# A one-core decoder block: reads of accumulators reordered, feature-major matmuls grouped by width, one gate block moved

## The chip, the cores and the metric

One core of a Trainium2 chip. The time is the device time of one execution in microseconds; lower is better. The kernel before took 669.32 us in the median of three runs (668.25 to 670.68).

## The reference

A decoder block over 256 tokens of width 2,048, float32 throughout. The input is RMS-normalised and goes through one wide projection, whose columns feed two mixers. One is an mLSTM with 4 heads of 256 (q and k pass a causal convolution of four taps and a SiLU, then chunks with gates); the other is sparse attention with 16 heads of 64 over 4 key groups (a compressed branch, a selected branch and a window branch). Each result is gated, both are joined, projected, and added to x.

```python
h = rmsnorm(x, norm_g[l])
(mq, mk, mv, mo, mz, mi, mf, nq, kc, vc, ks, vs, kw, vw, ng, nz) = split_cols(h @ w_in[l], IN_SPLITS)
...
hm = head_layernorm(hm, m_norm_g[l]).astype(x.dtype)
m_out = hm * jax.nn.sigmoid(mo) * jax.nn.silu(mz)
...
n_out = n_att * jax.nn.silu(nz)
x = x + jnp.concatenate([m_out, n_out], axis=-1) @ w_out[l]
ple = rmsnorm(p[l] @ ple_proj_w[l], ple_norm_g[l])
x = x + jax.nn.sigmoid(x @ ple_gate_w[l]) * ple
return rmsnorm(x, final_norm_g)
```

## The kernel before

**Blocks and units.** All weights are streamed once from DRAM in an order laid out by hand (`STREAM`, lines 54 to 65): cs, q0 to q2, kw, vw, mo, mv, qk0 to qk7, mz0 and mz1, then ple and nz in turn, out, gate. A block is a set of columns over the whole contraction; it is cut into units of one, two or four 128-row slices (`ku`). A unit is loaded on SP's queue (`load`, L155), split into a high part by ScalarE (L164) and a low part, the rest, by VectorE (L165), and multiplied by TensorE (`mm`). Each float32 product is made of three matmuls: high by high, high by low, low by high.

**Two forms.** A token-major block has the activations as the stationary operand and the weights as the moving one, up to 512 columns wide (L190). A feature-major block (qk0 to qk7, nz0 to nz3) has the weights stationary: per slice one matmul of 512 columns (high weights, both halves of the activations, L178) and one of 256 (low weights, high half, L179), in turn:

```python
for j in range(b.ku):
    ...
    PE.matmul(o, wh, b.xT(kt, True), start=kt == 0, stop=False, skip_group_check=True)
    PE.matmul(o[:, 0], wl, b.xT(kt)[0], start=False, stop=kt == b.nk - 1, skip_group_check=True)
```

**The order of the work.** The main loop (L1291) is one step per unit. A step evacuates the block that ended, loads the unit four ahead, splits the unit three ahead, multiplies its own unit, and calls `advance`, which gives every open track one turn, up to its next `yield`. Every engine runs its instructions in the order in which the steps issue them. Weights have four buffers, accumulators of the main kind three banks, of the aux kind two, of the wide kind one; two engines that read one accumulator tile are ordered one after the other as the program names them.

**The steps that matter here.**
- x_squares (L260) loads x in eight pieces on SP and squares them on ScalarE; norm_scale (L272) makes of the sums the scale rr (a power on GpSimd, L275) and its copies rh, rq and rb. The track starts in step 1, rope_tables (L326, a sine on ScalarE at L347) in step 11, split_w1 (L481, eight slices of the compression weights, L485 and L486) in step 15.
- After block cs, in step 16, split_v (L514) evacuates two accumulators: ScalarE reads the value half (L518), VectorE reads it (L519), then ScalarE reads the key half (`also`, L527). k_stack (L366) rotates the keys, splits them one step later into kst (L371, L372), and transposes them two steps after that (L383).
- nsa (L590) runs the attention in twelve rounds of five steps: scores, masked maximum (L695), exponentials (L706), a scaling on GpSimd (L717) that VectorE's L714 and L715 prepare, transposes (L729), the product with v.
- ev_qk and conv (L865, L882) evacuate a qk block and apply the convolution, mostly on VectorE (L893).
- mlstm (L918) starts after the last convolution. Per head there are three steps: e1 the exponentials, p1 the product into the wide bank (with p0, the scores of the next head), e2 the copy to hm (L963) and the statistics read from PSUM (L966, L967). Then all heads are normalised.
- ev_mz (L1014) evacuates an mz block and gate_m (L1029) multiplies the gates; when the heads are done it multiplies hm, transposes it in two groups (L1048) and evacuates each into mixm with ScalarE (L1053) and VectorE (L1054) in turn, each of the two groups of mz0 and mz1 through one aux bank.

## Time and profile before

| what | us |
|---|---|
| median of three runs | 669.32 |
| the profiled execution's own time | 668.31 |
| its span, first to last instruction | 666.6 |
| TensorE matmul busy (PE) | 645.2 |
| VectorE (DVE) / ScalarE (ACT) / GpSimd (POOL) busy | 456.0 / 378.6 / 62.6 |
| VectorE low parts of the weights, L165 | 258.6 |
| ScalarE high parts of the weights, L164 | 216.7 |

Matmuls are pipelined and their ends are modelled, so the busy time of TensorE overstates how long one takes; the distance between starts says more. PEld is the weight load, which overlaps. A number in brackets behind a timeline row is the idle time of the engine before it and what ended it. PEclk is the granted TensorE clock as a share of full speed.

### The profile page before, as it was taken

What the parts mean: (1) busy time and instruction counts of PE and PEld (TensorE: products, weight loads), DVE (VectorE), ACT (ScalarE), POOL (GpSimd) and SP (SyncE); (2) the same over time, 40 slices, a digit from 0 to 9 for tenths busy, and PEclk for the clock granted to TensorE, in tenths of its full rate; (3) what the DMA queues carried; (4) which work ended last, traced back from release to release, by engine and by line L of the source; (5) the groups of instructions that cost most, each with busy time, mean ns of one, the idle gap of its engine ahead of it and who ended that gap; (6) DMA issues with size and microseconds to landing.
All of it is one profiled execution on the core that took longest, in us unless ns stands there. A gap on an engine that the chain in (4) does not pass through costs nothing.

```text
span 666.6 us, 9325 instructions
## 1 busy us (share of the span) xinstructions
PE 645.2 (97%) x3423; PEld 555.6 (83%) x3423; DVE 456.0 (68%) x690; ACT 378.6 (57%) x647; POOL 62.6 (9%) x70
## 2 busy tenths in 40 slices
PE   7998999999999999999999999989999999999994
PEld 5887999998888888888878888868888888888884
DVE  4657788648666667999998565866655764545564
ACT  5757854665655547776666455667644434344442
POOL 0010230000111211111100000100000000022430
PEclk9999999999999999999999999989999999999998
DMA  8974555564555544444456535436588675566623
GB/s 286 387 284 140 165 174 168 150 213 147 169 154 160 160 139 147 137 149 134 150 176 192 186 126 156 154 115 207 179 273 297 197 235 180 186 188 191 188 96 127
DMA packets 36478, 121.05 MB, mean 182 GB/s; under 512 B 4304, under 2 KB 5072, under 8 KB 35920
## 3 DMA queue, kind: packets, MB, share of 16 engines
q1 hardware_dynamic: 35280, 115.98, 54.7%
q10 hardware_dynamic: 1152, 4.47, 1.9%
q8 instruction: 27, 0.44, 0.3%
q14 instruction: 19, 0.16, 0.1%
HBM read 118.33 MB, written 2.10 MB: 181 GB/s over the span
## 4 chain that ended last, share of the span: by engine, by line
PE 84%; DVE 8%; ACT 3%; issue 2%; DMA 1%; POOL 1%; SPq 0%; ACTq 0%; POOLq 0%
PE mainps L190 56%; PE mainps L178 10%; PE mainps L179 5%; DVE wlo L165 3%; PE wideps L190 3%; PE wideps L683 2%; PE auxps L729 1%; ACT whi L164 1%; DMA wraw<-in_wst_dram 1%; PE wideps L958 1%; PE po L762 1%; PE po L760 1%; PE auxps L1185 1%; PE auxps L933 1%; PE wideps L622 1%
## 5 line engine op out<-in xcount | busy, mean ns | idle before, releaser
L165 DVE TENSOR_TENSOR wlo<-wraw,whi 128x1024 fp32r<-128x1024 f32 (+3 forms) x218 | 258.6, 1187 | 175.5 <-ACT whi L164 171.7
L164 ACT CAST whi<-wraw 128x1024 fp32r<-128x1024 f32 (+3 forms) x218 | 216.7, 998 | 173.0 <-PE mainps L190 118.2
L190 PE MATMUL mainps<-whi,hT 128*128 128x512 f32 (+3 forms) x768 | 185.0, 361 | 2.9 <-ACT whi L164 1.4
L190 PEld LDWEIGHTS mainps<-whi,hT 128*128 128x128 f32 x768 | 131.1, 188 | 20.9 <-ACT whi L164 2.3
L178 PE MATMUL mainps<-hT,whi 128*128 128x512 f32 x384 | 137.6, 400 | 0.3 <-ACT ple L1109 0.3
L179 PE MATMUL mainps<-hT,wlo 128*128 128x256 f32 x384 | 107.9, 281 | 0.0
L190 PE MATMUL mainps<-wlo,hT 128*128 128x512 f32 (+3 forms) x384 | 106.6, 356 | 0.5 <-DVE wlo L165 0.5
L178 PEld LDWEIGHTS mainps<-hT,whi 128*128 128x128 f32 x384 | 72.5, 189 | 17.5 <-ACT ple L1109 0.6
L190 PEld LDWEIGHTS mainps<-wlo,hT 128*128 128x128 f32 x384 | 68.3, 188 | 9.9 <-DVE wlo L165 1.0
L179 PEld LDWEIGHTS mainps<-hT,wlo 128*128 128x128 f32 x384 | 72.8, 190 | 0.4
L190 PE MATMUL mainps<-whi,x2T 128*128 128x512 f32 (+1 forms) x288 | 70.4, 366 | 0.0
L190 PEld LDWEIGHTS mainps<-whi,x2T 128*128 128x128 f32 x288 | 50.8, 189 | 8.7
L717 POOL TENSOR_TENSOR pr<-pr,st 128x1024 f32<-128x1024 f32 x12 | 23.3, 1944 | 219.1 <-DVE st L715 219.1
L190 PE MATMUL mainps<-wlo,x2T 128*128 128x512 f32 (+1 forms) x144 | 41.0, 366 | 0.0
L190 PE MATMUL mainps<-whi,mixm 128*128 128x512 f32 x128 | 35.5, 399 | 0.0
L190 PE MATMUL mainps<-whi,mixn 128*128 128x512 f32 x128 | 34.2, 389 | 0.0
L190 PEld LDWEIGHTS mainps<-wlo,x2T 128*128 128x128 f32 x144 | 26.0, 189 | 4.5
L190 PEld LDWEIGHTS mainps<-whi,mixn 128*128 128x128 f32 x128 | 24.0, 188 | 5.1
L190 PEld LDWEIGHTS mainps<-whi,mixm 128*128 128x128 f32 x128 | 23.5, 188 | 5.1
L706 ACT ACTIVATE pr<-wideps,st 128x128 f32<-128x128 f32 (+1 forms) x64 | 26.5, 435 | 0.6 <-DVE st L695 0.6
L878 ACT COPY sc<-mainps 128x512 f32<-128x512 f32 x24 | 14.1, 586 | 17.5 <-PE mainps L179 17.4
L893 DVE SCALAR_TENSOR_TENSOR qk<-cv,csb,qk 128x253 f32<-128x253 f32 (+2 forms) x48 | 23.1, 481 | 1.1
(277 smaller groups left out, 707.5 us busy)
## 6 DMA issues: line engine op xcount, KB each, us to landing
wraw<-in_wst_dram SPq DMA_DIRECT2D x183, 512.0 KB, 3.7
wraw<-in_wst_dram SPq DMA_DIRECT2D x24, 344.0 KB, 3.2
wraw<-in_wst_dram SPq DMA_DIRECT2D x8, 304.0 KB, 2.9
xq<-in_x_dram SPq DMA_DIRECT2D x8, 256.0 KB, 8.5
w1raw<-in_w_dram SPq DMA_DIRECT2D x2, 1024.0 KB, 10.2
x<-in_x_dram ACTq DMA_DIRECT2D x4, 512.0 KB, 6.2
out_dram<-x SPq DMA_DIRECT2D x8, 256.0 KB, 2.7
xf<-in_xT_dram SPq DMA_DIRECT2D x3, 512.0 KB, 8.0
```

The costliest lines, as they stand in the source:

```text
L164: A.copy(hi[:, a:z], raw[:, a:z])
L165: V.tensor_tensor(lo[:, a:z], raw[:, a:z], hi[:, a:z].bitcast(F32), OP.subtract)
L178: PE.matmul(o, wh, b.xT(kt, True), start=kt == 0, stop=False, skip_group_check=True)
L179: PE.matmul(o[:, 0], wl, b.xT(kt)[0], start=False, stop=kt == b.nk - 1, skip_group_check=True)
L190: PE.matmul(b.ps[n], xx, (self.hi, self.lo)[part == 2][:, j, a:z], start=kt + part == 0, stop=part == 2 and kt == b.nk - 1)
L622: PE.matmul(psc[:, t, h].rearrange("p a c -> p (a c)"), qT[:, h, t * 128:(t + 1) * 128], kcmpT[:, h // NJ].rearrange("p a c -> p (a c)"), ...
L683: PE.matmul(ps[:, j], qT[:, g * NJ + j0 + j, t * 128:nk], kT[:, g, hl, :, 0:nk], start=hl == 0, stop=hl == 1)
L706: A.activation(d["pr"][:, j, b], d["ps"][:, j, b], AF.Exp, bias=st[:, 0, j, b:b + 1], accum_out=st[:, 1, j, b:b + 1])
L717: G.tensor_tensor(pf, pf, d["st"][:, 2].rearrange("p j b -> p (j b)")[:, :, None].to_broadcast([128, 2 * jn, nk]), OP.mult)
L729: PE.transpose(pt[:, s, j], d["pr"][:, j, b, s * 128:(s + 1) * 128], ident)
L878: A.copy(sc, ps[m])
L893: V.scalar_tensor_tensor(y[:, d:S], a[:, 0:S - d], w(j), y[:, d:S], op0=OP.mult, op1=OP.add)
```

## The change

Nine edits. In `mm`, the four slices' wide matmuls of a feature-major unit come first, then the four narrow ones. In split_v the call `also` stands before VectorE's read, and in gate_m both ScalarE reads stand before both VectorE reads. k_stack has one more yield before kst. The block mz0 moves ahead of the qk blocks, and the track ple_in opens with mz1. In mlstm the copy of a head is issued together with the exponentials of the next, its statistics are read from the SBUF copy hm one step later, and a head takes two steps. x_squares starts in step 3, rope_tables in step 10, split_w1 in step 13. The mv tile is 2,112 words instead of 2,056, and lg moves from the constants into the slot of bst.

```diff
@@ -56,8 +56,9 @@
 STREAM += [("kw", "w_in", span(C_KW, 256), KT, 4), ("vw", "w_in", span(C_VW, 304), KT, 2)]
 STREAM += [(f"mo{i}", "w_in", span(C_MO + i * 512, 512), KT, 2) for i in range(2)]
 STREAM += [(f"mv{i}", "w_in", span(C_MV + i * 512, 512), KT, 2) for i in range(2)]
+STREAM += [("mz0", "w_in", span(C_MZ, 512), KT, 2)]
 STREAM += [(f"qk{i}", "w_in", span(C_MQ + i * 256, 256), KT, 4) for i in range(8)]
-STREAM += [(f"mz{i}", "w_in", span(C_MZ + i * 512, 512), KT, 2) for i in range(2)]
+STREAM += [("mz1", "w_in", span(C_MZ + 512, 512), KT, 2)]
 for i in range(4):
     STREAM += [(f"ple{i}", "ple_proj_w", span(i * 512, 512), 2, 2)]
     STREAM += [(f"nz{i}", "w_in", span(C_NZ + i * 256, 256), KT, 4)]
@@ -171,12 +172,13 @@
             if b.feat:
                 for m in range(b.W // 128):
                     o = b.ps[m]
-                    for j in range(b.ku):
-                        kt = self.ka + j
-                        wh = self.hi[:, j, m * 128:(m + 1) * 128]
-                        wl = self.lo[:, j, m * 128:(m + 1) * 128]
-                        PE.matmul(o, wh, b.xT(kt, True), start=kt == 0, stop=False, skip_group_check=True)
-                        PE.matmul(o[:, 0], wl, b.xT(kt)[0], start=False, stop=kt == b.nk - 1, skip_group_check=True)
+                    ks = range(self.ka, self.ka + b.ku)
+                    for j, kt in enumerate(ks):
+                        PE.matmul(o, self.hi[:, j, m * 128:(m + 1) * 128], b.xT(kt, True), start=kt == 0, stop=False,
+                                  skip_group_check=True)
+                    for j, kt in enumerate(ks):
+                        PE.matmul(o[:, 0], self.lo[:, j, m * 128:(m + 1) * 128], b.xT(kt)[0], start=False,
+                                  stop=kt == b.nk - 1, skip_group_check=True)
                 return
             ns = range(len(b.cuts)) if ns is None else ns
             order = [(n, part) for n in ns for part in range(3)]
@@ -366,6 +368,7 @@
     def k_stack(kx, b):
         rope(kx.rearrange("p t (g d) -> p t g d", d=ND), NG)
         yield
+        yield
         kst = tmp.tile([128, T * NG, 2, 2, ND], F32R, name="kst", tag="hm")
         kb = kx.rearrange("p t (g d) -> p (t g) d", d=ND)[:, :, None, :].to_broadcast([128, T * NG, 2, ND])
         A.copy(kst[:, :, 0], kb)
@@ -516,9 +519,9 @@
         for t in range(T):
             v = ps_v[t].rearrange("p (g d) -> p g d", d=ND)
             A.activation(vs[:, t, :, 0], v, AF.Copy, scale=rr[:, t:t + 1])
+            also(t)
             V.scalar_tensor_tensor(vs[:, t, :, 1], v, rr[:, t:t + 1], vs[:, t, :, 0].bitcast(F32),
                                    op0=OP.mult, op1=OP.subtract)
-            also(t)
         vst[b] = vs
 
     def ev_s(ps):
@@ -807,7 +810,7 @@
         zz = zif.rearrange("p t (a h) -> p t a h", a=2)
         V.tensor_tensor(zz, zz, b_if[:, None].to_broadcast([128, T, 2, MH]), OP.add)
         zf = zz[:, :, 1]
-        lg = const.tile([128, 4, T, MH], F32, name="lg")
+        lg = tmp.tile([128, 4, T, MH], F32, name="lg", tag="bst")
         e, u, u2, ac = (lg[:, i] for i in range(4))
         V.scalar_tensor_tensor(e, zf, -1.0, zf, op0=OP.mult, op1=OP.max)
         A.activation(e, e, AF.Exp, scale=-1.0)
@@ -899,13 +902,16 @@
         if i == 7:
             tracks.append(mlstm())
 
+
+    MV_WORDS = 2112
     mv = None
 
     def ev_mv(i):
         def f(ps):
             nonlocal mv
             if i == 0:
-                mv = tmp.tile([128, T, MH, MD + 1], F32, name="mv", tag="mv")
+                mv = tmp.tile([128, MV_WORDS], F32, name="mv", tag="mv")[:, 0:T * MH * (MD + 1)]
+                mv = mv.rearrange("p (t h d) -> p t h d", t=T, h=MH)
                 G.memset(mv[:, :, :, MD:MD + 1], 1.0)
             for t in range(T):
                 A.activation(mv[:, t, 2 * i:2 * i + 2, 0:MD], ps[t].rearrange("p (h d) -> p h d", d=MD), AF.Copy,
@@ -962,21 +968,28 @@
             pn = sv[h]
             A.copy(hm[:, :, h], pn[:, :, 0:MD])
             V.tensor_copy(den[:, 0, :, h:h + 1], pn[:, :, MD:MD + 1])
+
+        def e3(h):
             for t in range(T):
-                V.bn_stats(bst[:, t, h], pn[:, t, 0:MD])
+                V.bn_stats(bst[:, t, h], hm[:, t, h])
                 V.bn_aggr(mva[:, t, h], bst[:, t, h])
 
         p0(0)
         yield
         for h in range(MH):
+            if h:
+                e2(h - 1)
             e1(h)
             yield
             p1(h)
             if h + 1 < MH:
                 p0(h + 1)
-            yield
-            e2(h)
-            yield
+            if h:
+                e3(h - 1)
+            yield
+        e2(MH - 1)
+        e3(MH - 1)
+        yield
         dd, rv, sh = den[:, 0], den[:, 1], den[:, 2]
         V.scalar_tensor_tensor(dd, dd, -1.0, dd, op0=OP.mult, op1=OP.max)
         V.tensor_scalar(dd, dd, 1.0, None, op0=OP.max)
@@ -1048,10 +1061,10 @@
                     PE.transpose(ps[:, j, t * 128:(t + 1) * 128], hf[:, t, (k0 + j) * 128:(k0 + j + 1) * 128], ident)
             yield
             for j in range(2):
-                hi, lo = mixm[:, 0, k0 + j], mixm[:, 1, k0 + j]
-                g = mgcol[:, k0 + j:k0 + j + 1]
-                A.activation(hi, ps[:, j], AF.Copy, scale=g)
-                V.scalar_tensor_tensor(lo, ps[:, j], g, hi.bitcast(F32), op0=OP.mult, op1=OP.subtract)
+                A.activation(mixm[:, 0, k0 + j], ps[:, j], AF.Copy, scale=mgcol[:, k0 + j:k0 + j + 1])
+            for j in range(2):
+                V.scalar_tensor_tensor(mixm[:, 1, k0 + j], ps[:, j], mgcol[:, k0 + j:k0 + j + 1],
+                                       mixm[:, 0, k0 + j].bitcast(F32), op0=OP.mult, op1=OP.subtract)
         done.add(f"mix{i}")
 
     def ev_nz(i):
@@ -1258,14 +1271,14 @@
     pb = [Block(f"ple{i}", ev_ple(i), p_of) for i in range(4)]
     mo, mz, nz = ([Block(f"{c}{i}", f(i), h_of, feat=c == "nz") for i in range(n)]
                   for c, f, n in (("mo", ev_mo, 2), ("mz", ev_mz, 2), ("nz", ev_nz, 4)))
-    blocks += mo + mv_b + qk_b + mz
+    blocks += mo + mv_b + mz[0:1] + qk_b + mz[1:2]
     for i in range(4):
         blocks += [pb[i], nz[i]]
     blocks += [Block(f"out{i}", ev_out(i), mix_of) for i in range(4)]
     blocks += [Block(f"gate{i}", ev_gate(i), x2_of, cuts=EDGES if i == 3 else None) for i in range(4)]
     assert [woff[n] for n, *_ in STREAM] == [b.off for b in blocks]
     units = [Unit(b, ka) for b in blocks for ka in range(0, b.nk, b.ku)]
-    ple_first = next(i for i, u in enumerate(units) if u.b is mz[0])
+    ple_first = next(i for i, u in enumerate(units) if u.b is mz[1])
     NU = len(units)
 
     first = ((512, 768), (768, 1024), (0, 512))
@@ -1304,15 +1317,16 @@
             load_x(8 + 4 * (i // 4), 12 + 4 * (i // 4))
             if i == 1:
                 nc.sync.dma_start(pos_i, positions)
-                tracks.append(x_squares())
+        elif i == 3:
+            tracks.append(x_squares())
         elif i in (6, 9):
             load_w1(i // 3 - 2)
-        elif i == 11:
+        elif i == 10:
             tracks.append(rope_tables())
         elif i == 12:
             nc.sync.dma_start(csb[:, 16:], cols[:, 16:N_COLS - 3 * ND])
             nc.sync.dma_start(boot, cols[:, N_COLS - 3 * ND:])
-        elif i == KT - 1:
+        elif i == 13:
             tracks.append(split_w1(w1r))
         elif i == KT + 2:
             tracks.append(masks())
```

## Rows read from the trace of the kernel before

**Rows 1.** The page, part 1: busy us (share of the span) xinstructions.

```profile
PE 645.2 (97%) x3423; PEld 555.6 (83%) x3423; DVE 456.0 (68%) x690; ACT 378.6 (57%) x647; POOL 62.6 (9%) x70
```

**Rows 2.** Windows: length, busy us (x) of each engine, PEclk, DMA share, GB/s.

```profile
52.00:56.00 4.00, 2.87 (x17) 2.46 (x16) 2.85 (x6) 1.95 (x6) 0.00 (x0) 1.00 0.83 240
140.00:332.00 192.00, 192.00 (x1043) 164.90 (x1042) 146.70 (x206) 119.55 (x254) 21.20 (x12) 1.00 0.49 152
332.00:336.00 4.00, 2.67 (x19) 2.21 (x18) 3.97 (x6) 3.10 (x5) 2.18 (x1) 1.00 0.57 182
436.00:440.00 4.00, 1.04 (x6) 0.68 (x6) 2.92 (x6) 2.11 (x5) 0.00 (x0) 0.83 0.68 227
440.00:444.00 4.00, 4.00 (x19) 3.59 (x20) 3.42 (x6) 1.45 (x4) 0.00 (x0) 0.74 0.22 45
```

**Rows 3.** Chain of waits: start us, us, what; 256-column kw, then 512-column blocks.

```profile
111.99 11.57 PE mainps L190 x96
...
145.78 2.84 PE mainps L190 x12
...
359.68 10.90 PE mainps L190 x48
```

**Rows 4.** Waits: engine line waited for: us in total, times, longest us.

```profile
ACT trig L347 <- DVE akk L345: 3.7, 1, 3.7
...
ACT kx L527 <- DVE vst L519: 2.0, 2, 1.5
```

**Rows 5.** Timeline of TensorE, block nz0: start us, us, engine line op [idle before].

```profile
417.52 0.39 PE L178 MATMUL mainps<-hT,whi 128*128 128x512 f32 x1
...
428.81 1.11 PE L190 MATMUL mainps<-whi,pTt 128*128 128x512 f32 x4
```

**Rows 6.** Timeline 44 to 65 us, GpSimd, ScalarE, VectorE, TensorE.

```profile
46.34 0.71 POOL L275 TENSOR_TENSOR rr<-rr,mh 128x2 f32<-128x2 f32 x1 [44.97 <-DVE posf L328]
...
52.44 0.47 ACT L518 ACTIVATE vst<-mainps,rr 128x256 fp32r<-128x256 f32 x1
...
53.90 0.47 DVE L519 SCALAR_TENSOR_TENSOR vst<-mainps,rr,vst 128x256 fp32r<-128x256 f32 x1
...
54.40 0.47 ACT L527 ACTIVATE kx<-mainps,rr 128x256 f32<-128x256 f32 x1 [1.50 <-DVE vst L519]
...
57.59 0.79 ACT L164 CAST whi<-wraw 128x688 fp32r<-128x688 f32 x1
...
62.79 1.22 DVE L372 TENSOR_TENSOR kst<-kx,kst 128x1024 fp32r<-128x1024 f32 x1
...
64.07 0.37 PE L383 MATMUL auxps<-identr,kst 128*128 128x128 f32 x2 [1.83 <-DVE kst L372]
```

**Rows 7.** Timeline 332 to 336 us, VectorE and TensorE.

```profile
333.12 2.92 DVE L165 TENSOR_TENSOR wlo<-wraw,whi 128x1024 fp32r<-128x1024 f32 x1
...
335.01 1.09 PE L729 MATMUL auxps<-ident,pr 128*128 128x128 f32 x8 [1.33 <-POOL pr L717]
```

**Rows 8.** Timeline at the joint of mz0 and mz1, VectorE and TensorE.

```profile
387.40 0.69 DVE L1022 SCALAR_TENSOR_TENSOR tz<-tz,zc 128x512 f32<-128x512 f32 x1 [0.49 <-ACT zc L1021]
...
387.42 1.20 PE L190 MATMUL mainps<-whi,hT 128*128 128x512 f32 x4 [0.34 <-ACT zc L1021]
```

**Rows 9.** Timeline of VectorE, statistics of the last head.

```profile
412.97 0.42 DVE L966 BATCH_NORM_STATS2 bst<-wideps 128x6 f32<-128x256 f32 x1
```

**Rows 10.** Timeline 436 to 440 us, VectorE, ScalarE, TensorE.

```profile
436.90 0.48 DVE L1054 SCALAR_TENSOR_TENSOR mixm<-auxps,csb,mixm 128x256 fp32r<-128x256 f32 x1
437.41 0.84 ACT L1053 ACTIVATE mixm<-auxps,csb 128x256 fp32r<-128x256 f32 x2 [1.31 <-DVE mixm L1054]
437.92 0.88 DVE L1054 SCALAR_TENSOR_TENSOR mixm<-auxps,csb,mixm 128x256 fp32r<-128x256 f32 x2 [0.54 <-ACT mixm L1053]
...
438.55 0.99 PE L1048 MATMUL auxps<-ident,hm 128*128 128x128 f32 x4 [2.53 <-DVE mixm L1054]
...
439.96 1.08 PE L1048 MATMUL auxps<-ident,hm 128*128 128x128 f32 x4 [0.43 <-DVE mixm L1054]
```

## The prediction

> **What bounds the kernel now.** I read the page first: the matmul stream is busy for 645.2 of 666.6 us [rows 1]. The four-microsecond windows come second, because a share over the whole span hides the places where TensorE stands still. From 140 to 332 us TensorE has no idle time at all; the windows that matter are those that fall short [rows 2]. In 52-56 us 1.13 us are missing, in 332-336 us 1.33, in 436-440 us 2.96, and the window after that is full but was granted a clock of 0.74 in the mean, so part of it ran on the lower level of 1.2 GHz. With the wait of 1.83 us at 64 us [rows 6] those holes, some 7.3 us and a slow stretch behind the last, are what a reordering can win in the middle of the run. Elsewhere only fewer matmul nanoseconds would help, and those are read from the chain of waits: 48 matmuls of 512 columns in 10.90 us, 227 ns each, and 96 of 256 columns in 11.57 us, 120.5 ns each [rows 3].
>
> The waits [rows 4] name what ended an engine's idle time, and the timelines further down show in which order it came about.
>
> **The matmuls sorted by width.** Alternating, the 32 pairs of block nz0 start at 417.52 us and are followed at 428.81 us: 11.29 / 32 = 352.8 ns a pair [rows 5]. Runs of one width would cost 227 + 120.5 = 347.5 ns [rows 3]. There are 12 feature-major blocks of 32 pairs, so 384 x 5.3 ns = 2.0 us, if every neighbour had its own width. In a group of four and four two of eight joints still change width, so I take less than three quarters: **-1.4 us**, between -2.0 and +1.7 (if the wide ones then run as in the slower dozen of rows 3, 2.84 / 12 = 237 ns: 384 x 4.4 ns more than now). A second effect costs no matmul time: the first narrow matmul, which needs the low half from VectorE, moves back by three wide ones, 3 x 227 = 0.68 us of slack for a late VectorE.
>
> The Trainium skill, page "TensorE: Matmul & The Clock Gate", section "Back-to-back issue gap", gives N / 2.4 + 2.5 ns for a matmul on the full clock, 215.7 + 109.2 = 325 ns a pair in either order. By it this term would be zero and the sum 1.4 us higher; both rows lie above it, and the measured 352.8 against 347.5 decides.
>
> **The front, 52 to 64 us.** Today ScalarE reads the value half of an accumulator, VectorE reads it, and only then may ScalarE read the key half: kx waits 1.50 us for vst, the second time 0.5 more, 2.0 us in two waits [rows 4, 6]. TensorE's second q0 matmul group waits for the bank that this read frees. With both ScalarE reads first, the bank is free when the vst subtraction ends, 53.90 + 0.47 = 54.37 instead of 54.40 + 0.47 = 54.87, and ScalarE reaches the cast that stands at 57.59 us [rows 6] 2.0 us sooner. That cast is what VectorE idles for, and the key split kst (62.79 to 64.01) follows it without a gap. TensorE has waited 1.83 us for it when its transposes go on at 64.07 us [rows 6]. The added yield of k_stack makes the split come one unit later on ScalarE and VectorE (one weight split and one w1 slice, about 1.4 us of VectorE, go ahead of it) and the transposes one unit later on TensorE (12 matmuls of 344 columns, about 1.9 us); alone it gains some 0.5 us, with the 2.0 us of ScalarE it leaves nothing to wait for.
> The moved tracks point the same way. The rope tables' sine, for which ScalarE stands 3.7 us [rows 4], comes one step earlier, into time in which VectorE idles; the w1 slices start two steps earlier; the rb copy goes from ahead of the vst subtraction to behind it. The price is that the squares of x, their eight 256 KB loads on SP's queue and with them the scale rr come two steps later. The loads fall behind two weight loads that are needed sooner, so SP's queue loses nothing. GpSimd makes rr at 46.34 + 0.71 = 47.05 us; two steps of 12 wide matmuls (2.72 us each) later is 52.5, and the evacuation that reads it starts at 52.44 [rows 6]. That is no cover at today's pace; but VectorE's step 13, where rr is then made, runs late today behind ScalarE's 3.7 us stand, which goes, so I expect some 2 us of cover. Beyond it each microsecond would stand on TensorE. I take **-2.7 us** of the 1.13 + 1.83; bounds -3.0 and +0.5 (rr a microsecond late, and only the bank's earlier release won).
>
> **mz0 ahead of qk.** Eight units of 2.72 us go ahead, with their eight loads (1,024 elements a partition each, as qk's) in the same order on SP; no matmul is added. The attention steps, one step later through k_stack, then overlap some seven steps less with the convolution. In that overlap VectorE is full (3.97 of 4) and falls behind until TensorE waits 1.33 us for a GpSimd product whose scalars came late [rows 2, 7]; there too a split took 2.92 us beside GpSimd's. With the overlap 7 x 2.7 us shorter the lag should not get there: **-1.3 us**, bounds -1.4 and +1.3 (it happens once more, since mz0's own work now lies in the attention: four ScalarE reads and four VectorE products of 0.69 us [rows 8], in the first two steps of qk, where VectorE is not yet full and the units of 2.8 us cover them). At the joint of mz0 and mz1 TensorE waits 0.34 us for a copy that stood behind the exponentials of a mixed head [rows 8]; that joint is gone and the new ones have one more bank's time: **-0.3 us**.
>
> **The heads and the mix.** A head now takes two steps instead of three, and its statistics read the SBUF copy. One from PSUM takes 0.42 us [rows 9]; no row shows one from SBUF. All eight lie beside matmuls, so up to twice that or half of it costs nothing; were they uncovered, they would cost up to 3.4 us. The end of the heads comes three steps earlier, but the transposes of the mix meet the next ple block instead of this one, in the same place of the same five-step pattern. So I expect the hole again, shorter. Now its four evacuations alternate, ScalarE, VectorE, ScalarE, VectorE, each waiting for the other: TensorE, done with its matmuls at 436.0, goes on at 438.55 and again at 439.96 [rows 10]. With both ScalarE reads first, VectorE can run its four subtractions of 0.4 us (two take 0.88) from 436.90 on without a wait, done near 438.7: **-1.2 us**. Bounds 0 and -4.5 (the hole of 2.96 gone, and with it the slow clock behind it, 0.74 of full speed over 4 us [rows 2], worth about a microsecond of matmuls).
>
> The padded mv tile, the lg tile in a pool slot, and the gates read ahead of the split in vw change no queue that anything waits on: zero, covered by full TensorE windows.
>
> **Sum.** -1.4 - 2.7 - 1.3 - 0.3 - 1.2 = -6.9 us against the profiled execution's own 668.3 us: 661.4. That execution lies 1.0 us below the median of the runs shown (669.32), so on the median's side I predict **662.4 us**.
>
> **Rivals.**
> 1. The waits are not from the order of readers but from VectorE's load, so the order of reads alone wins nothing: kx then still waits, kst too. Against it stands that VectorE is named as the releaser of a ScalarE read of other columns [rows 4]. The front keeps -0.5, the mix 0: 662.4 + 2.2 + 1.2 = 665.8 us. Chance 0.15.
> 2. Holes move. VectorE's lag in the overlap of convolution and attention recurs at each of the roughly five remaining attention rounds, 1.3 us each, in place of the one: 662.4 + 1.3 + 5 x 1.3 = 670.2, about no change. For it: VectorE is full there [rows 2]. Against: with as much overlap the rounds before the last one passed without a hole, 140 to 332 us. Chance 0.10, counting smaller forms of it.
> 3. Slower: the padded tile moves every later buffer, and the wide matmuls read their operands more slowly. Place: all 1,536 token-major matmuls of 512 columns. Price: the same twelve take 2.84 us in one stretch and 12 x 227 = 2.72 in another [rows 3], 0.12 x 128 twelves = 15.4 us: 677.8. It decides from 0.055 us a twelve on, where it eats the whole gain. Against it: both values stand in one trace, in which no buffer moves. Chance 0.05.
> 4. The hole at the mix vanishes and the clock stays full: 662.4 - 3.3 = 659.1. Chance 0.15.
>
> **How the numbers follow.** The forecast itself has 0.55. The range reaches from rival 4 with the better end of the sorting, 658, to rival 1 and part of rival 2, 667; about 0.15 lies above it, 0.04 below. A measurement of this kernel can tell about 0.3% (2.0 us) from no change. Faster by more than that: forecast, rivals 1 and 4, a little of rival 2, 0.86; within it 0.08; slower 0.06.
>
> **What would show it.** In the profile after: kx no longer waits for vst; the windows from 52 to 64 us read nearly 4.00; no wait of the probability transposes for the GpSimd product; eight matmuls of a feature-major group in about 1.39 us instead of 1.41; the second transposes of the mix come about 1.2 us after the first's request, not 4. I am wrong if a window that is full now shows a hole, above all where rr is first read and in the heads under nz0, or if twelve wide matmuls take over 2.75 us throughout.

## The result, and the profile after

The changed kernel takes **657.62 us** in the median of four runs (657.20 to 658.03), beside 669.81 (668.25 to 670.68) for the kernel before on the same chip: a ratio of 0.9821, with an interval of 0.9800 to 0.9841. That is 12.2 us less; 6.9 were forecast, and the time lies 0.4 us under the low end of the range. The profiled execution took 657.20 us, span 655.2.

Page, part 1, of the changed kernel (answers to [rows 1]):

```profile
PE 641.0 (98%) x3423; PEld 554.7 (85%) x3423; DVE 456.1 (70%) x690; ACT 379.0 (58%) x647; POOL 62.5 (10%) x70
```

The same instructions on every engine, and 4.2 us less matmul busy time, so 7.2 of the 11.4 us of span are idle time that went. Windows (answer to [rows 2]):

```profile
50.00:54.00 4.00, 4.00 (x25) 3.65 (x24) 2.83 (x6) 3.85 (x11) 2.59 (x11) 1.00 0.67 208
58.00:62.00 4.00, 4.00 (x29) 3.98 (x29) 4.00 (x6) 3.08 (x6) 0.00 (x0) 1.00 0.61 176
140.00:330.00 190.00, 190.00 (x1006) 162.39 (x1005) 139.58 (x190) 116.49 (x246) 22.06 (x13) 1.00 0.49 152
330.00:334.00 4.00, 3.44 (x24) 2.98 (x23) 3.93 (x5) 1.65 (x3) 1.31 (x1) 1.00 0.45 141
440.00:444.00 4.00, 2.67 (x18) 2.15 (x16) 3.13 (x6) 4.00 (x9) 0.00 (x0) 1.00 0.46 150
444.00:448.00 4.00, 3.86 (x25) 3.54 (x26) 3.96 (x8) 3.23 (x7) 0.00 (x0) 1.00 0.60 156
```

Both holes of the front are gone, the one near 330 us is smaller (0.56 for 1.33), and the mix misses 1.47 us where it missed 2.96, with the full clock behind it. Timelines of the front, ScalarE, GpSimd, VectorE and TensorE (answer to [rows 6]):

```profile
45.43 0.22 ACT L349 ACTIVATE trig<-akk 128x32 f32<-128x32 f32 x1
...
49.65 0.47 ACT L521 ACTIVATE vst<-mainps,rr 128x256 fp32r<-128x256 f32 x1
50.02 0.46 ACT L530 ACTIVATE kx<-mainps,rr 128x256 f32<-128x256 f32 x1
...
48.00 1.09 POOL L277 TENSOR_TENSOR rr<-rr,mh 128x2 f32<-128x2 f32 x1 [46.63 <-DVE rr L276]
...
59.72 1.22 DVE L375 TENSOR_TENSOR kst<-kx,kst 128x1024 fp32r<-128x1024 f32 x1
...
61.13 0.45 PE L386 MATMUL auxps<-identr,kst 128*128 128x128 f32 x4
```

The sine and kx carry no bracket: nobody waits any more ([rows 4] had 3.7 and 2.0 us there). The scale rr is ready at 49.09, 0.56 us ahead of the first evacuation that reads it. TensorE asks for kst after it is done, 60.94. Then the wait near 330 us and the mix, TensorE, ScalarE and VectorE (answer to [rows 7, 10]):

```profile
331.36 1.09 PE L732 MATMUL auxps<-ident,pr 128*128 128x128 f32 x8 [0.56 <-POOL pr L720]
...
438.72 0.60 PE L1061 MATMUL auxps<-ident,hm 128*128 128x128 f32 x4
442.08 0.60 PE L1061 MATMUL auxps<-ident,hm 128*128 128x128 f32 x4
444.14 0.63 PE L1061 MATMUL auxps<-ident,hm 128*128 128x128 f32 x4 [1.47 <-DVE mixm L1066]
...
441.83 0.85 ACT L1064 ACTIVATE mixm<-auxps,csb 128x256 fp32r<-128x256 f32 x2
442.56 1.06 ACT L165 CAST whi<-wraw 128x1024 fp32r<-128x1024 f32 x1
443.49 0.87 ACT L1064 ACTIVATE mixm<-auxps,csb 128x256 fp32r<-128x256 f32 x2
...
441.98 1.22 DVE L166 TENSOR_TENSOR wlo<-wraw,whi 128x1024 fp32r<-128x1024 f32 x1 [0.87 <-ACT whi L165]
443.12 0.87 DVE L1066 SCALAR_TENSOR_TENSOR mixm<-auxps,csb,mixm 128x256 fp32r<-128x256 f32 x2
```

The order on each engine is as planned, ScalarE twice, then VectorE twice. But the two gate tracks now run a step apart: the one of mz0 stands ahead of the heads' track in the list and sees its end a step later. So three groups want two banks within two steps, and the third waits until VectorE, behind a weight split, has emptied one.

**Where the time went.** Read from the timelines as distances between the first matmuls of stages, which no modelled end can blur: start-up (to the fourth unit of cs), front (from there to mv1), middle (mv1 to out0) and end (out0 to the last matmul).

| kernel | start-up | front | middle | end | own time |
|---|---|---|---|---|---|
| before | 16.85 | 205.79 | 255.19 | 179.52 | 668.31 |
| changed | 15.80 | 201.30 | 250.28 | 178.59 | 657.20 |
| e1_pad | 15.59 | 206.98 | 256.49 | 178.60 | 668.62 |
| e2_nopad | 16.21 | 201.27 | 250.31 | 179.51 | 658.26 |
| e3_reads | 16.64 | 203.13 | 253.05 | 179.52 | 663.29 |
| e4_tracks | 16.96 | 202.97 | 257.11 | 179.50 | 667.50 |
| e9_splitback | 15.63 | 204.46 | 250.28 | 178.58 | 659.93 |
| e10_tracksback | 15.39 | 203.18 | 249.88 | 178.59 | 657.99 |
| e5_nosort | 17.11 | 201.48 | 250.25 | 178.59 | 658.55 |
| e6_mzback | 16.42 | 201.38 | 249.85 | 178.58 | 657.35 |
| e8_mixback | 16.38 | 201.27 | 252.44 | 178.59 | 660.07 |
| e7_headsback | 16.56 | 201.26 | 252.55 | 178.55 | 660.22 |
| e12_lockstep | 15.79 | 201.25 | 250.13 | 178.58 | 656.89 |
| e13_apart | 16.37 | 201.38 | 248.51 | 178.59 | 655.92 |
| e15_lgonly | 17.66 | 206.87 | 254.40 | 179.49 | 669.23 |
| e16_pad2080 | 15.98 | 201.32 | 250.52 | 179.62 | 658.57 |
| e18_shift32 | 15.48 | 201.95 | 250.28 | 178.58 | 657.31 |
| e19_movr | 15.95 | 199.74 | 249.61 | 178.59 | 654.97 |
| e20_after (the changed kernel again) | 16.22 | 202.22 | 250.27 | 178.59 | 658.36 |
| e21_best (e19 again) | 15.87 | 200.28 | 249.58 | 178.59 | 655.57 |

The change is -1.05, -4.49, -4.91 and -0.93 us. The start-up follows no edit: 15.39 to 17.66 over these executions, 15.80 and 16.22 for the changed kernel itself. The end is good to 0.1 us. The front and the middle repeat as closely where the waits and the clock are the same (nine executions with the changed front take 201.25 to 201.48 us); where they are not, the traces show two reasons.

- The clock behind a hole. The front of e1 and e15, in which it is unchanged, takes 206.98 and 206.87 us instead of 205.79, although TensorE's waits there are as long or shorter. Behind the wait for kst the granted clock was 0.81 and 0.76 in e1 (60 to 64 and 64 to 68 us) and 0.57 in e15 (64 to 68 us); in the kernel before it was 1.00. The middle of the four kernels with the old mix, 254.40 to 257.11, scatters in the main for the same reason, behind the mix (see e8).
- A load that lands late. Near 42 us a cast of ScalarE waits for a weight load in every execution (2.35 us in the changed kernel and in e20). It starts 9.2 to 10.2 us ahead of q0's first matmul in those nine, but 8.71 in e18 and 8.38 in e20. There the queues of ScalarE and VectorE are late behind it, TensorE waits 0.40 and 0.71 us for VectorE's vst, and the front is 201.95 and 202.22 us. The scale rr comes through the same queues and was ready 0.03 us ahead of the first evacuation that reads it. TensorE in e20:

```profile
53.39 0.90 PE L192 MATMUL mainps<-whi,hT 128*128 128x344 f32 x4 [0.71 <-DVE vst L523]
```

### The profile page after: what moved, and what is told of

Its sections match the earlier page's. It is cut to its first block, busy times and chain, and to the rows that moved or that the text cites. A ratio compares the mean times of both kernels' runs of the same rounds, so it can differ in the third digit from the quotient of the medians.

```text
span 655.2 us, 9343 instructions
## 1 busy us (share of the span) xinstructions
PE 641.0 (98%) x3423; PEld 554.7 (85%) x3423; DVE 456.1 (70%) x690; ACT 379.0 (58%) x647; POOL 62.5 (10%) x70
## 4 chain that ended last, share of the span: by engine, by line
PE 90%; DVE 5%; issue 2%; DMA 1%; ACT 1%; SPq 0%; POOL 0%; POOLq 0%; ACTq 0%; DVEq 0%
PE mainps L192 60%; PE mainps L177 12%; PE mainps L180 6%; PE wideps L192 3%; DVE wlo L166 2%; PE wideps L686 2%; PE auxps L732 1%; DMA wraw<-in_wst_dram 1%; PE wideps L964 1%; PE po L765 1%; PE po L763 1%; PE auxps L1198 1%; PE auxps L939 1%; PE wideps L625 1%; DVE kcs L412 1%
## 5 line engine op out<-in xcount | busy, mean ns | idle before, releaser
L177 PE MATMUL mainps<-hT,whi 128*128 128x512 f32 x384 | 105.6, 396 | 0.0
L177 PEld LDWEIGHTS mainps<-hT,whi 128*128 128x128 f32 x384 | 66.1, 189 | 9.3
L180 PEld LDWEIGHTS mainps<-hT,wlo 128*128 128x128 f32 x384 | 58.8, 189 | 8.2
L180 PE MATMUL mainps<-hT,wlo 128*128 128x256 f32 x384 | 61.0, 281 | 0.0
```

The lines of the kernel that those rows point to most:

```text
L177: PE.matmul(o, self.hi[:, j, m * 128:(m + 1) * 128], b.xT(kt, True), start=kt == 0, stop=False, skip_group_check=True)
L180: PE.matmul(o[:, 0], self.lo[:, j, m * 128:(m + 1) * 128], b.xT(kt)[0], start=False, stop=kt == b.nk - 1, skip_group_check=True)
```

## The experiments

The theory: most of the gain is waits that the reordered reads took away, plus a layout effect; the rivals are named in each expectation.

**The layout: pad and lg alone (e1), the changed kernel without them (e2).**

```diff
-                mv = tmp.tile([128, T, MH, MD + 1], F32, name="mv", tag="mv")
+                mv = tmp.tile([128, MV_WORDS], F32, name="mv", tag="mv")[:, 0:T * MH * (MD + 1)]
...
-        lg = const.tile([128, 4, T, MH], F32, name="lg")
+        lg = tmp.tile([128, 4, T, MH], F32, name="lg", tag="bst")
```

> The kernel before with the wider mv tile and the moved lg tile alone. Theory layout (later buffers lie elsewhere, and the matmuls of the out and gate blocks read them faster): from the start of out0 to the last matmul 178.6 us as after the change instead of 179.5, the time 0.9 us lower, perhaps with the start 1 us earlier. Rival chance (both differences are from one execution to the next): 179.5 us as before, no difference that repeats.

> The changed kernel with the old mv and lg tiles. Theory layout: out0 to the last matmul 179.5 us again, the time 0.9 us above the changed kernel's 657.6. Rival chance: 178.6 us, the same time.

e1 took 667.76 us, 0.9974 of before (0.9952 to 0.9996); e2 658.84, 0.9859 (0.9835 to 0.9884). The end stage decides it: 178.60 us with the layout edits, 179.51 without, whatever else the kernel has. So the two edits that I had costed at nothing are worth 0.9 us, in the four out blocks.

**Why: lg alone (e15), another size (e16), everything 32 bytes later (e18).**

```diff
e15: lg in the slot of bst, mv as before
e16: -    MV_WORDS = 2112
     +    MV_WORDS = 2080
e18: +    gap = const.tile([128, 8], F32, name="gap")
```

> The kernel before with lg in the slot of bst alone: weight buffers and everything behind them start 128 bytes earlier, mixm and the tiles behind mv too. Measured from the first matmul of out0 to the end (179.5 us before, 178.6 with both layout edits): if the start of mixm modulo 64 bytes decides (it stays a multiple of 64 here), 179.5; if the place of the weight buffers decides, 178.6.

> The changed kernel with the mv tile at 2,080 words instead of 2,112: mixm starts 32 bytes ahead of where it was before instead of 96 bytes behind, so an odd multiple of 32 as in the changed kernel, but at another distance from the weight buffers. If the start modulo 64 bytes decides, the stretch from out0 to the end is 178.6 us; if the size of 2,112 words or the distance to the weight buffers decides, 179.5.

> The changed kernel with one more unread constant of 32 bytes ahead of nearly all tiles, so that the weight buffers, mv, mixm and mixn all start 32 bytes later and keep their distances. If the distance of mixm from the weight buffers (equal places modulo 256 bytes) makes the four out blocks faster, the stretch from out0 to the end stays 178.6 us; if the absolute place of mixm decides, it goes to 179.5.

End stage: 179.49, 179.62 and 178.58 us. One tile, mixm on TensorE: instruction and count, shortest, median and longest ns, then first and last start. First the changed kernel:

```profile
L192 PE MATMUL mainps<-whi,mixm x128: 387/389/481, 467.4 to 545.8; 128*128 128x512 f32 x128
```

e15, e16 and e18:

```profile
L190 PE MATMUL mainps<-whi,mixm x128: 389/395/483, 478.9 to 558.3; 128*128 128x512 f32 x128
```
```profile
L192 PE MATMUL mainps<-whi,mixm x128: 387/395/477, 467.8 to 547.2; 128*128 128x512 f32 x128
```
```profile
L192 PE MATMUL mainps<-whi,mixm x128: 387/389/481, 467.7 to 546.1; 128*128 128x512 f32 x128
```

192 matmuls by 5 ns or so make the 0.9 us. From the program's allocation of tiles, the start of mixm less that of the weight buffers, modulo 256 bytes, is 0 in the three fast layouts (changed, e1, e18) and 32, 32, 32 and 128 in the slow ones (before, e2, e15, e16); the sizes of mv, 8,448, 8,224 and 8,320 bytes, leave the same remainders. The start modulo 64 bytes, my first theory, fell with e16; the absolute place of mixm fell with e15 and e18 (128 bytes ahead of its old place and 128 behind, the same modulo 256, and only e18 is fast); the place of the weight buffers fell with e15, where it is that of the changed kernel. That the stationary operand should start at the same place modulo 256 bytes as the moving one fits all seven, but other distances were not tried.

**The front: the reads alone (e3), the tracks and the yield alone (e4), and each undone in the changed kernel (e9, e10).**

```diff
             A.activation(vs[:, t, :, 0], v, ...)
+            also(t)
             V.scalar_tensor_tensor(vs[:, t, :, 1], v, ...)
-            also(t)
```
```diff
-                tracks.append(x_squares())
+        elif i == 3:
+            tracks.append(x_squares())
...
-        elif i == 11:
+        elif i == 10:
...
-        elif i == KT - 1:
+        elif i == 13:
...
         yield
+        yield
         kst = ...
```

The first edit, with the order of reads at the mix, makes e3 of the kernel before, and undone alone makes e9 of the changed one; the second makes e4 and, undone, e10.

> The kernel before with only the order of the reads changed, in the evacuation after cs and in the mix. Theory order (each ScalarE read stood behind a VectorE read of the same accumulator tile): kx waits no more, the wait of TensorE for kst falls from 1.8 us to under 0.5, q1's start comes about 2 us earlier by this alone; the hole at the mix falls by 1.2 us; together about 3.5 us. Rival load (VectorE is late anyway): kst still ends where it did, q1's start moves by under 0.7 us, and the mix hole by under 0.5.

> The kernel before with only the moved tracks and the added yield of k_stack. Theory order: the wait for kst shrinks by about 0.5 us only, kx still waits 1.5 us for vst, q1's start moves by under 1 us. Rival load: the tracks free VectorE and ScalarE before the evacuation, and the hole at 61 to 64 us goes without the reads: q1's start moves by 2.5 us or more. If the squares start later and the first loads gain by it, the start of continuous matmuls moves from 14.45 to about 13.4 us; otherwise that is chance.

> The changed kernel with the old order of reads in split_v alone. From the first matmul of q0 to that of the second unit of q1: 22.62 us before, 19.30 after, 20.93 with the moved tracks alone, 20.00 with the reads alone. If the two edits of the front add up by half, this one loses what the tracks alone lacked, 1.6 us: about 659.3 us and a stretch of 20.9. If the tracks and the added step already cover the reads, the stretch stays under 19.8 and the time under 658.2.

> The changed kernel with the tracks of x, the tables and the w1 slices in their old steps and without the added step of k_stack. As the reads alone gave 20.00 us in that stretch, 0.7 us is lost there: about 658.3 us. If the later k_stack and attention are also what shrank the wait for the probability product near 330 us from 1.5 to 0.7 us, another 0.6 to 0.8 is lost in that place: about 659.0. If the tracks are worth nothing beside the reads, 657.6.

The front falls by 2.7 us with the reads and by 2.8 with the tracks, alone; undone, it grows by 3.2 and 1.9. Together they bring 4.5. So each is worth 2 to 3 us in this stage, and neither closes both holes: with the reads alone TensorE still waits 0.27 and 0.40 us (e3), with the tracks alone the first wait is gone and 1.50 us of the second is left (e4). Not all that the tracks win in the front is kept: without them (e10) the middle is 0.40 us shorter, and in e4 it is 1.9 us longer than before, 1.1 of it in qk4 to qk6 and 0.7 behind the mix. TensorE in e3, in e4, and ScalarE and TensorE in e9:

```profile
53.85 0.89 PE L190 MATMUL mainps<-whi,hT 128*128 128x344 f32 x4 [0.27 <-DVE vst L520]
...
61.22 0.37 PE L383 MATMUL auxps<-identr,kst 128*128 128x128 f32 x2 [0.40 <-DVE kst L372]
```
```profile
63.97 0.36 PE L384 MATMUL auxps<-identr,kst 128*128 128x128 f32 x2 [1.50 <-DVE kst L373]
```
```profile
52.73 0.47 ACT L530 ACTIVATE kx<-mainps,rr 128x256 f32<-128x256 f32 x1 [2.48 <-DVE vst L522]
...
53.26 0.90 PE L192 MATMUL mainps<-whi,hT 128*128 128x344 f32 x4 [1.17 <-ACT kx L530]
64.12 0.36 PE L386 MATMUL auxps<-identr,kst 128*128 128x128 f32 x2 [1.55 <-DVE kst L375]
```

With the tracks moved and the old order of reads both holes of [rows 6] are back: the releaser was rightly named, and rival 1 falls. The front's loss, 3.2 us, is more than the 2.7 that the two brackets add up to.

**The sorting undone (e5).**

```diff
-                    for j, kt in enumerate(ks):
-                        PE.matmul(o, self.hi...)
-                    for j, kt in enumerate(ks):
-                        PE.matmul(o[:, 0], self.lo...)
+                    for j in range(b.ku):
+                        PE.matmul(o, wh...)
+                        PE.matmul(o[:, 0], wl...)
```

> The changed kernel with wide and narrow matmuls of a feature-major unit in turn again. If sorting is worth what single starts show, a group of eight takes 1.43 us instead of 1.41 and the twelve blocks together 1.6 us more: about 659.2 us against 657.6, spread evenly over qk and nz. If the sorting's worth lay in the later use of the low half, a wait of TensorE for VectorE's split comes back in the qk blocks and the loss is 3 us or more in one place. If it is worth nothing, 657.6 plus or minus 0.5.

Its own time is 1.35 us longer, but 1.31 of that is start-up; the other three stages add up to 0.15 us, and that lies in the front, where no feature-major block runs (the middle is 0.03 us shorter). None of the three expectations is met as put: the loss is nothing, yet the pace does differ. Timeline of TensorE in e5, eight pairs apart, in qk6 and in nz3:

```profile
353.41 0.39 PE L179 MATMUL mainps<-hT,whi 128*128 128x512 f32 x1
...
356.19 0.39 PE L179 MATMUL mainps<-hT,whi 128*128 128x512 f32 x1
...
459.30 0.40 PE L179 MATMUL mainps<-hT,whi 128*128 128x512 f32 x1
...
462.13 0.40 PE L179 MATMUL mainps<-hT,whi 128*128 128x512 f32 x1
```

And the changed kernel, a unit (eight pairs, sorted) apart:

```profile
458.96 1.09 PE L177 MATMUL mainps<-hT,whi 128*128 128x512 f32 x4
...
461.77 1.09 PE L177 MATMUL mainps<-hT,whi 128*128 128x512 f32 x4
```

Eight alternating pairs take 2.78 us in one place and 2.83 in another; eight sorted ones 2.81 in all twelve units of qk5 to qk7. In e5 the twelve units of qk5 to qk7 ran at the better pace, which is why sorting gained nothing on it. In the kernel before nearly all ran at 2.83, two units behind the mix at 2.77. So sorting was worth some 46 x 0.02 = 0.9 us against that execution, and nothing against this one.

**mz0 behind qk again (e6).**

```diff
-    blocks += mo + mv_b + mz[0:1] + qk_b + mz[1:2]
+    blocks += mo + mv_b + qk_b + mz
```

> The changed kernel with mz0 behind the qk blocks again, as before. If the place of the gate track in the list matters (mz0's gates then stand behind the heads' track again, both gates see its end in one step), eight transposes of the mix come in one step and the second groups wait for both banks: a hole of 1.9 us and a small second one instead of one of 1.5. The hole behind the last attention round and the convolutions grows from 0.7 to 1.3 us again and the joint of mz0 and mz1 waits 0.3 to 0.6 again: 657.6 + 0.6 + 0.6 + 0.5, about 659.3 us. If the block's place is only about VectorE's load, the mix keeps its one hole and the sum is 658.7.

Neither: the middle is 0.43 us *shorter* than in the changed kernel. The waits in the overlap come back in part (units of 4.21, 4.74 and 4.38 us between qk4 and qk6, where the changed kernel has one of 4.37), but the mix has no hole at all. TensorE there:

```profile
418.41 0.60 PE L1060 MATMUL auxps<-ident,hm 128*128 128x128 f32 x4
...
428.08 0.60 PE L1060 MATMUL auxps<-ident,hm 128*128 128x128 f32 x4
```

With mz0 late and the short heads, the heads end while VectorE still multiplies the gates of mz1, whose groups so come two steps behind mz0's, and the four spread over 10 us. So moving mz0 won at its own places and lost it again at the mix: nothing in the sum.

**The order of reads at the mix undone (e8).**

```diff
-            for j in range(2):
-                A.activation(mixm[:, 0, k0 + j], ps[:, j], ...)
-            for j in range(2):
-                V.scalar_tensor_tensor(mixm[:, 1, k0 + j], ps[:, j], ...)
+            for j in range(2):
+                A.activation(hi, ps[:, j], ...)
+                V.scalar_tensor_tensor(lo, ps[:, j], ...)
```

> The changed kernel with the mix evacuations alternating ScalarE, VectorE, ScalarE, VectorE again, while the two gate tracks stay a step apart. If the order of the reads made the gain at the mix, its hole grows from 1.5 to about 2.7 us and the time to 658.8 us or more. If the step between the two tracks made it, four evacuations of different steps have room enough and the hole stays within 0.4 us of 1.5: 657.6 to 658.0.

The middle grows by 2.16 us, of which the order of reads has 0.63 in the hole, even with the tracks a step apart. ScalarE, VectorE, TensorE, and the window behind:

```profile
444.19 0.47 ACT L1066 ACTIVATE mixm<-auxps,csb 128x256 fp32r<-128x256 f32 x1 [1.32 <-DVE mixm L1067]
...
444.70 0.48 DVE L1067 SCALAR_TENSOR_TENSOR mixm<-auxps,csb,mixm 128x256 fp32r<-128x256 f32 x1 [0.54 <-ACT mixm L1066]
...
445.33 1.09 PE L1061 MATMUL auxps<-ident,hm 128*128 128x128 f32 x4 [2.10 <-DVE mixm L1067]
```
```profile
444.00:448.00 4.00, 2.67 (x9) 2.32 (x10) 3.42 (x6) 1.78 (x3) 0.00 (x0) 0.65 0.43 137
```

The rest is the clock, granted at 0.65 behind it, so partly on the 1.2 GHz level. The reads alone (e3) show the same from the other side: they take 2.1 us off the middle, of which the two waits of TensorE are 1.0 (the hole measured from start to start less its matmuls: 2.69 and 0.74 us before, 2.08 and 0.32 in e3) and the clock the rest.

That the clock falls behind such a hole is not certain. In e15, which has the old mix, TensorE stood as long as before and the full clock was granted behind it. TensorE in e15, and the window behind:

```profile
440.48 0.63 PE L1048 MATMUL auxps<-ident,hm 128*128 128x128 f32 x4 [2.55 <-DVE mixm L1054]
```
```profile
442.00:446.00 4.00, 4.00 (x25) 3.54 (x25) 3.42 (x6) 1.38 (x4) 0.00 (x0) 1.00 0.19 41
```

With the two waits alike (3.3 to 3.7 us together, from start to start), block nz1, in which the mix lies, took 16.53 us in e15, 17.35 before (clock 0.74 in the window behind), 18.09 in e4 (0.77) and 18.81 in e1 (0.50). Against e15 the 15.26 us of e3 are 1.3 less, and nearly all of that is the waits. So the order of reads wins some 0.6 to 1.3 us of waits, and beside them up to some 2.5 us of clock in some executions and none in others. e3, ScalarE, VectorE, TensorE, window:

```profile
432.70 1.58 ACT L1051 ACTIVATE mixm<-auxps,csb 128x256 fp32r<-128x256 f32 x4
...
433.99 1.65 DVE L1053 SCALAR_TENSOR_TENSOR mixm<-auxps,csb,mixm 128x256 fp32r<-128x256 f32 x4
...
435.00 0.63 PE L1048 MATMUL auxps<-ident,hm 128*128 128x128 f32 x4 [1.92 <-DVE mixm L1053]
```
```profile
432.00:436.00 4.00, 1.93 (x13) 1.34 (x12) 3.16 (x6) 3.54 (x7) 0.00 (x0) 1.00 0.66 181
```

The four subtractions run without a wait, as predicted, and the clock behind stays full.

**The long heads again (e7).**

```diff
-                V.bn_stats(bst[:, t, h], hm[:, t, h])
+                V.bn_stats(bst[:, t, h], pn[:, t, 0:MD])
...
-            if h:
-                e2(h - 1)
             e1(h)
...
-            if h:
-                e3(h - 1)
-            yield
-        e2(MH - 1)
-        e3(MH - 1)
-        yield
+            yield
+            e2(h)
+            yield
```

> The changed kernel with three steps a head and statistics read from PSUM again. If the shorter head is what lets the mix go on with a smaller hole than the order of reads alone explains, the transposes come some 8 us later, the hole at the mix grows from 1.5 us to 2 or more, and the time is 658.2 to 659.5 us. If the shorter head only moves the mix to another place of the same pattern, the time stays within 0.4 us of 657.6, wherever the hole then lies.

The middle grows by 2.27 us, but not at the mix, whose hole is down to 0.55: the heads now reach into nz0 and nz1. TensorE and ScalarE in e7:

```profile
427.57 1.21 PE L177 MATMUL mainps<-hT,whi 128*128 128x512 f32 x4 [1.24 <-ACT ple L1115]
...
425.58 0.40 ACT L952 ACTIVATE ee<-em,gc 128x128 f32<-128x128 f32 x1 [1.74 <-DVE em L949]
...
426.95 1.05 ACT L1115 COPY ple<-mainps 128x512 f32<-128x512 f32 x2
```

TensorE waits for the copy that empties ple's bank, and that copy stands behind a head's exponentials, which had waited 1.74 us for VectorE. The shorter head is worth 2.3 us in this kernel, with the full clock behind its holes too, and I had costed it at nothing. The statistics have no part in it; VectorE in the changed kernel, from the SBUF copy:

```profile
400.57 0.42 DVE L974 BATCH_NORM_STATS2 bst<-hm 128x6 f32<-128x256 f32 x1
```

0.42 us, as from PSUM [rows 9].

**The step between the gate tracks: none (e12) and two (e13).**

```diff
e12:          while "mlstm" not in done:
                  yield
     +        if i == 1:
     +            yield
e13: +        if i == 0:
     +            yield
     ...
     -        if i == 0:
     +        if mixm is None:
                  mixm = tmp.tile(...)
```

> The changed kernel with one more step of waiting for the gates of mz1, so that both gate tracks run in step as they did before, with the new order of reads. If the step between them made part of the gain, eight transposes come in one step, the second groups wait for both banks, and the mix loses 0.6 to 1.5 us: 658.2 to 659.1 us, with a hole of about 2 us. If only the order of reads counts, the hole stays 1.5 us and the time 657.6.

> The changed kernel with the gates of mz0 one step later still, so that the two gate tracks run two steps apart and each bank's evacuation has a step of its own. If the remaining hole of 1.5 us comes from two groups wanting both banks in one step, it goes: 656.0 us. If it comes from VectorE being full while block nz0 is evacuated, the hole only moves and the time stays within 0.4 us of 657.6.

Without the step the mix waits 0.73 and 0.16 us instead of 1.47, so the step apart was no gain: that theory fell. With two steps the hole is gone, as the first theory of e13 had it. e12 and e13, TensorE, and e13's window:

```profile
446.37 0.63 PE L1063 MATMUL auxps<-ident,hm 128*128 128x128 f32 x4 [0.73 <-DVE mixm L1068]
447.15 0.63 PE L1063 MATMUL auxps<-ident,hm 128*128 128x128 f32 x4 [0.16 <-DVE mixm L1068]
```
```profile
442.60 0.60 PE L1063 MATMUL auxps<-ident,hm 128*128 128x128 f32 x4
445.84 0.60 PE L1063 MATMUL auxps<-ident,hm 128*128 128x128 f32 x4
```
```profile
440.00:444.00 4.00, 4.00 (x25) 3.48 (x24) 3.13 (x5) 4.00 (x9) 0.00 (x0) 1.00 0.57 198
```

What remained at the mix was groups of two tracks wanting both banks at once; VectorE was as full in e13 (3.13 of 4 us in this window, as in the changed kernel).

**A version that beats the changed kernel (e19, e20, e21).** e13 with one more `yield` ahead of the compression's matmuls, which waited 0.73 us there for movr (0.76 in the changed kernel); then the changed kernel and this one, on one chip, in five rounds.

> The kernel with the two gate tracks two steps apart and one more step between movr's low half and the matmuls that read it. If that step only takes away the wait of 0.76 us near 86 us, 655.2 us. If the later compression moves the attention a step and with it the overlap with the convolutions, the wait near 330 us or the mix changes by up to 1.5 us in either direction: 654 to 657.5.

> The changed kernel once more, beside the next one on the same chip: 657.6 us, 0.982 of the kernel before.

> The kernel with the gate tracks two steps apart and the later matmuls of the compression once more, on the same chip as the changed kernel. From the first matmul of q0 to the end it was 2.2 us shorter than the changed kernel in single executions, so 655.4 us, and faster than the changed kernel by 0.3%. If start-up chance made that difference, both are alike within 0.5 us.

e19 took 655.67 us (654.89 to 657.30). Side by side, e20 took 657.97 (656.88 to 658.36), 0.9839 of before (0.9816 to 0.9862), and e21, the same as e19, 655.53 (654.97 to 656.46), 0.9804 (0.9779 to 0.9830). The runs of the two do not overlap: 2.4 us less in the medians. Of the 2.2 us that single executions promised, the added yield brought less than its wait: the front of e19 is 1.6 us shorter than that of e13, its middle 1.1 longer, and in e21 both are 1.1. What the yield is worth by itself is not shown. What the second step between the gate tracks is worth is: block nz2, in which the mix now lies, takes 12.59 us in e13, e19 and e21 and 14.35 in both executions of the changed kernel.

## Why the prediction was too small

The time fell below the range because three terms were mis-sized: the front brought -4.5 us instead of -2.7, the mix -3.3 instead of -1.2, and the layout -0.9 where nothing was put.

- **The front (-2.7 us, bounds -3.0 and +0.5) was the largest miss: -4.5.** The places, releasers and order were right, and e3, e4 and e9 show that both edits were needed to close both holes. The bound failed: I took the idle times 1.13 + 1.83 = 2.96 as all there was to win. From q0's first matmul to the second unit of q1 it went from 22.62 to 19.30 us, 3.3 us, since idle time is counted from an end that is modelled, past the point where the next matmul could have started: from start to start, less the matmuls between, the two waits are 1.30 and 2.05 us. And the execution before was the better case: with the clock fallen behind the wait for kst, the same stretch took 23.93 us in e1 and 23.66 in e15. Another 0.5 us came out of cs (its fourth unit to q0, 35.84 to 35.36, with the moved tracks only) and 0.5 out of the mo blocks (53.95 to 53.40), where no window had shown a hole. The cover of rr, estimated at 2 us, was 0.56 us, and 0.03 in e18 and e20: there a hole did open where rr is first read, as I had named it for a sign of being wrong, but behind a late load.
- **The mix (-1.2 us) brought -3.3.** From ple1 to ple2 before 20.93 us, beside 14.07 for the clean stretch from ple3 to out0; from ple2 to ple3 after 17.48, beside 13.95. The excess fell from 6.86 to 3.53. The shorter hole by the order of reads was sized well (1.0 against 1.2). Two things were left out: the slow clock behind the hole, about another microsecond in the execution before, which I had bounded only for a hole that is gone, while behind the shorter one of e3 it was not slow either (rival 4 had half of this; in e15 the clock stayed full behind the long hole, so this microsecond was that execution's); and the shorter heads, costed at nothing because they "lie beside matmuls". Their matmuls hide them, but ScalarE's queue does not: a copy that empties a bank stands behind them (e7).
- **The padded tile and lg (zero) brought -0.9.** "Change no queue" was true and not the point: they change where mixm starts (e1, e2, e15, e16, e18). Rival 3 had the mechanism with the wrong sign, place and size: 192 matmuls of the out blocks, 5 ns faster each. Its price rested on a dozen of 2.84 us [rows 3] that shows no slower pace: its first four matmuls, behind narrow ones, took 1.01 us, the next four 0.91.
- **mz0 ahead (-1.3 and -0.3).** The wait near 330 us fell from 1.49 to 0.72 us between starts, -0.8, and the joint of mz0 and mz1 (0.50) is gone. But both were given back at the mix, and e6, with mz0 in the old place, is no slower. The argument was right at its places and missed that the gate track, now ahead of the heads' track in the list, falls out of step. Rival 2 did not come about: from 140 to 330 us TensorE has no idle time.
- **The sorting (-1.4, from -2.0 to +1.7)** was worth 0.9 against the alternating pace of the kernel before and nothing in e5. The price of a sorted pair was too low: runs of one width were to cost 347.5 ns, and 351 were measured; alternating ones took 347 to 354. The rule of the Trainium skill that I weighed ("TensorE: Matmul & The Clock Gate", section "Back-to-back issue gap") gives N / 2.4 + 2.5 ns as the gap of a matmul by itself, from which 325 ns a pair in either order is an estimate. The traces show no such pace.
- **Start-up.** 1.05 us of the difference between the two profiled executions follows no edit.
- The terms measured, -0.9, -4.5, -0.8, -0.5, -3.3 and -0.9, add up to -10.9 for the three stages, where -10.3 was measured; 0.6 us of small losses in the middle stay unassigned (the 0.40 of e10 is probably among them).

## What to carry to other kernels

Price a wait of TensorE by the distance between matmul starts less the matmuls in it, not by its idle time, and count the clock behind it as a loss that may come or not. When a track moves in the list of work, count again in which step it sees its flag and how many banks it then shares; a step more or less between two tracks was worth 1.8 us here (e13), at no cost. A pad that moves a stationary tile is an edit like any other: measure it alone.

## What the runs showed of the hardware

- The pace of 512-column matmuls depended on where the stationary tile lies: median 389 or 395 ns, 0.9 us over four blocks, with the distance to the weight buffers modulo 256 bytes 0 or not.
- Alternating wide and narrow matmuls ran at either of two paces, 2.78 or 2.83 us for eight pairs, within one execution (e5), and kept it over several blocks; the sorted ones ran at 2.81. What sets the pace was not found.
- The granted clock fell behind a hole in some executions and not in others, with holes of the same length. Behind the mix in its old order it was 0.74 before, 0.50 in e1, 0.77 in e4 and 0.65 in e8, where TensorE had stood for 2.53, 2.54, 2.53 and 2.10 us; it was 1.00 in e15, after 2.55. Behind the wait for kst, 1.83, 1.83 and 1.82 us, it was 1.00 before, down to 0.76 in e1 and 0.57 in e15. In all fifteen executions with the new order at the mix it was 1.00 there; the longest stand among them was the 1.92 us of e3. What decides is not shown.
